# Weight sums spread over the U stage, the first gate pair's front drawn into the last output pair, and a reordered last row in a one-core encoder block

## The chip, the cores and the metric

The kernel runs on one core of one Trainium2 chip. The metric is the device time of one execution in microseconds (us), the median of several executions. TensorE (PE) does the matmuls and transposes, VectorE (DVE) and ScalarE (ACT) the elementwise work, GpSimd (POOL) a few small powers and some table loads, and SyncE (SP) issues nearly all of the 176 MB of DMA.

## The reference, cut to what matters

One layer of an encoder for 512 prompt and 1024 sample rows of width 1024, all in float32:

```python
xn = rmsnorm(h, norm_mix_g)
q, k, v, g_att, u, g_f = split(xn @ w_in)        # six column groups of 512
att = diff_attention(q, k, v, lam, rel_bias)     # 4 heads, softmax(1) - lam * softmax(2)
att = rmsnorm(att, subln_g) * (1 - lambda_init) * silu(g_att)
fno = real(fft2(u per group)) @ w_fourier * silu(g_f)
h = h + concat(att, fno) @ w_out
h = h + sigmoid(rmsnorm(h, ple_norm_g) @ w_ple_gate) * (p @ w_ple_proj)
return rmsnorm(h, final_norm_g)
```

## The kernel before

Every float32 operand of a matmul is split into a high and a low part (`split`, L53: a cast on ACT, a subtraction on DVE), and each product is three matmuls. The 1536 rows are 12 tiles of 128, or three chunks of 512 columns. The Tile framework orders the instructions of each engine from the program's order and its own estimate of times, and gives out the buffers of a tag as they come free, so a load may stand well ahead of its place in the program.

The stages, in order of time:

- V (to about 82 us): the chunks are loaded, and the value columns computed.
- U (82 to 148 us): for each row tile t, 24 matmuls into one of two `acc` banks, an ACT multiply that empties the bank into `u`, and a store. After t = 3, 7, 11 `norm_in_place` (L326) normalizes a chunk (24 DVE and 8 ACT instructions). `combine` (L408) makes sums of weight quarters for a seven-product form of the 2x2 block product: two loads of 512 KB into a tile `wr`, four subtractions into a tile `f`, then for `w_out` (n = 0 to 3) four splits and four stores of `so`, for `w_ple_gate` (n = 4 to 7) two ACT multiplies by the norm's gain and two stores of `sg`. Before, `combine` 0 to 3 follow t = 1, 4, 7, 10.
- The first column blocks of q and k (148 to about 182 us): `columns_on` (L210) is a generator; `run(columns_on, 3)` advances it by one block and chunk, that is 24 matmuls. `blocks` loads the weights of the next block (`load_col`: tags `raw`, `wch`, `wcl`, two buffers each) when it begins a block. `combine` 4 to 7 each follow one of the first four such steps. After six steps the pool `pn` closes, and `pf` takes its memory: `fa` with rows of u, `cs` and `wf` with tables.
- The Fourier stage (to about 290 us), with more columns between its products, then attention (to about 669 us), with columns and the first two output tiles poured between its steps.
- The output projection: tiles 2 to 11 in pairs. `left` (L908) makes the seven left operands of a pair from four blocks `cl`, with temporaries f1, f2 from the tag `tmp` (two buffers, which tiles 0 and 1 use for their split columns `ch`). `project_pair` (L926) does the seven products of 12 matmuls into four banks, adds each to x, and `keep` stores the row and sums its squares, with `acc` banks as ACT's dummy output. At t = 4 the weights `wp` of p and the final gain `gfin` are loaded.
- The gate: `front` (L997) loads a pair of kept rows, normalizes them (`normed`, into a buffer of tag `hn`, which has four; the staging tiles `raw4` of all late weights share the tag), transposes them on PE (L993) and makes the left operands. `front(0)` begins after the last output pair and runs to its end between the loads of the second and third of the seven gate weights. `gate_pair` (L1068) does the products of one pair and the next pair's front; `finish_row` (L1047) ends each row.

In the last row `gfin` is multiplied in ahead of the final scale, in three pieces (L1109, L1116 twice), and the two halves leave through ACT's and SP's queues.

Of the kernel before, what the change touches and what calls it, by code (L numbers as in the profile page):

```python
# [15 lines left out]
D = 1024  # L16
# [16 lines left out]
def block_kernel(ctx, tc, i, yp, ys):  # L33
# [10 lines left out]
    def tr():  # L44
        return psum.tile([P, 512], F32, tag="tr", name="tr", bufs=2)
# [150 lines left out]
    def blocks(*todo):  # L196
# [7 lines left out]
        for n, (b, chunks) in enumerate(todo):  # L204
# [2 lines left out]
            w = nxt  # L207

    ALL = (0, 1, 2)
    columns_on = blocks(("k0 q0", (0, 1)), ("k0 q0", (2,)), ("g0 k1 q1 g1 k2 q2 g2 k3 q3 g3", ALL),  # L210
                        ("f0 f1 f2 f3", (0, 1)))

    def run(gen, n=None):
# [37 lines left out]
    with tc.tile_pool(name="pn", bufs=1, side="right", reuse_waits="tile") as pn:  # L251
# [156 lines left out]
        def combine(n):  # L408
            k, gate = n % 4, n // 4
            src = i["w_ple_gate" if gate else "w_out"][0]  # L410
            both = pn.tile([P, 4, 512], F32, tag="xs" if gate else "wn", name="wr", bufs=4)
            r = [both[:, 0:2], both[:, 2:4]]
            for j in range(2):
                b = 4 * j + k
                nc.sync.dma_start(out=r[j].rearrange("p a b -> p (a b)"), in_=src[b * P:(b + 1) * P, :])
                if gate:
                    nc.scalar.mul(out=r[j], in_=r[j], mul=gcol[:, b:b + 1])
            f = pn.tile([P, 4, 512], F32, tag="wn", name="f", bufs=4)
            t1, t2, t3, t4 = (f[:, z] for z in range(4))
            for out, x0, x1 in ((t1, r[0][:, 1], r[0][:, 0]), (t2, r[1][:, 1], t1),  # L420
                                (t3, r[1][:, 1], r[0][:, 1]), (t4, t2, r[1][:, 0])):
                nc.vector.tensor_tensor(out=out, in0=x0, in1=x1, op=ALU.subtract)
            if gate:
                for z in range(2):
                    nc.sync.dma_start(out=sums_g[z][:, :, k], in_=f[:, 2 * z:2 * z + 2])
            else:
                for m, t in zip(SUMS_R, (t1, t2, t3, t4)):
                    if m in ("t1", "t3"):
                        o2 = pn.tile([P, 4, 512], F32R, tag="wn", name="o", bufs=4)
                    o = o2[:, 0:2] if m in ("t1", "t3") else o2[:, 2:4]  # L430
                    split(o[:, 0], o[:, 1], t)
                    nc.sync.dma_start(out=sums_o[m][:, :, k], in_=o.bitcast(F32))

        wu = load_nat(2048, "xs")
        for t in range(NT):
            c, q = t // 4, (t % 4) * P
            ps = acc()
            for k in range(KB):
                x = [x[c][k // 4][:, k % 4, q:q + P] for x in (xh, xl)]
                mm3(ps, *x, wu[0][k // 4][:, k % 4], wu[1][k // 4][:, k % 4], k == 0, k == KB - 1)  # L440
            s, r = rows_of(t)
            u = px.tile([P, 512], F32, tag="th", name="u", bufs=3)
            nc.scalar.mul(out=u, in_=ps, mul=rs[c][:, t % 4:t % 4 + 1])
            nc.sync.dma_start(out=uu[s][r:r + P, :], in_=u)
            if t % 4 == 3:
                norm_in_place(c, rs[c])
            if t % 3 == 1:
                combine(t // 3)
        for n in range(6):
            run(columns_on, 3)  # L450
            if n < 4:
                combine(4 + n)


    with tc.tile_pool(name="pf", bufs=1, side="right", reuse_waits="tile") as pf:
# [427 lines left out]
    with ExitStack() as pcx:  # L883
# [21 lines left out]
        def add(out, x0, x1, eng=None):  # L905
            (eng or nc.vector).tensor_tensor(out=out, in0=x0, in1=x1, op=ALU.add)

        def left(cl):  # L908
            c11, c12, c21, c22 = cl
            a = {n: halves(n) for n in SUMS}  # L910
            a["11"] = a["11"][0], c11
            f11, f12, f21, f22 = (c.bitcast(F32) for c in cl)
            f1, f2 = tmp(), tmp()
            split(*a["12"], f12)
            split(*a["22"], f22)
            add(f1, f21, f22)
            split(*a["s1"], f1)
            sub(f2, f1, f11)
            split(*a["s2"], f2)
            sub(f2, f12, f2)  # L920
            split(*a["s4"], f2)
            sub(f1, f11, f21)
            split(*a["s3"], f1)
            return a, split_own(*a["11"])

        def project_pair(t, a, x):  # L926
            (xa, xb), L, R = x, slice(0, 512), slice(512, 1024)
            b0, b1, b2, b3 = banks(t)
            product(b0, a["11"], wb["11"], True)
            add(xa[:, L], b0, xa[:, L])  # L930
            product(b2, a["12"], wb["21"], True)
            add(xa[:, L], b2, xa[:, L])
            product(b3, a["22"], wb["t4"], True)
            sub(xb[:, L], xb[:, L], b3)
            product(b1, a["s1"], wb["t1"], True)
            add(xb[:, R], b1, xb[:, R])
            product(b0, a["s2"], wb["t2"], False)
            add(xa[:, R], b0, xa[:, R])
            product(b1, a["s4"], wb["22"], False)
            add(xa[:, R], b1, xa[:, R])  # L940
# [6 lines left out]
        def raw4():  # L947
            return pool.tile([P, D], F32, tag="hn", name="raw", bufs=4)

        a, (hi, lo) = left(pair_cl)  # L950
        with tc.issue_after(hi.ins), tc.issue_after(lo.ins):
            project_end(*later[0])
        for t in range(2, NT, 2):
            if t == 4:
                wp = [[pool.tile([P, D], F32R, tag=f"wp{k}{n}", name=f"wp{k}{n}") for n in "hl"]
                      for k in range(2)]
                gfin = pool.tile([P, D], F32, name="gfin")
                nc.scalar.dma_start(out=gfin, in_=i["final_norm_g"].rearrange(
                    "(a d) -> a d", a=1).broadcast_to([P, D]))
                for k in range(2):  # L960
                    raw = raw4()
                    nc.sync.dma_start(out=raw, in_=i["w_ple_proj"][0][k * P:(k + 1) * P, :])
                    split(*wp[k], raw)
            if t > 2:
                a, _ = left(load_cl(t, True))
            project_pair(t, a, [load_x(t, row(t)), load_x(t + 1, row(t + 1))])

        def rows_in(t):

# [27 lines left out]
        def front(t):  # L997
# [13 lines left out]
            pa = columns(pr, 0)  # L1011
            yield
            gb = normed(t + 1, xb)
            bank = tr if t else acc
            nc.scalar.copy(out=f21, in_=turn(gb, 0, bank()))
            ps = turn(gb, 1, bank())
            split(*a["22"], ps)
            add(f1, f21, ps)
            yield
# [27 lines left out]
        def finish_row(t, u, x, g, ss, n):  # L1047
            x, g, last = x[u], g[u], t + u == NT - 1
            rs = pool.tile([P, 1], F32, tag="rs", name="rs", bufs=2)
            nc.vector.tensor_reduce(out=rs, in_=ss[:, 4 * u:4 * u + n], op=ALU.add, axis=mybir.AxisListType.X)  # L1050
            rpow(rs, rs)
            t += u
            for z in range(2):
                w = slice(512 * z, 512 * z + 512)
                dst = yp[0, t * P:(t + 1) * P, w] if t < 4 else ys[0, (t - 4) * P:(t - 3) * P, w]
                if not last:
                    nc.vector.scalar_tensor_tensor(out=g[:, w], in0=x[:, w], scalar=rs, in1=gfin[:, w],
                                                   op0=ALU.mult, op1=ALU.mult)
                    nc.sync.dma_start(out=dst, in_=g[:, w])
                elif z == 0:  # L1060
                    nc.scalar.mul(out=g[:, w], in_=x[:, w], mul=rs)
                    nc.scalar.dma_start(out=dst, in_=g[:, w])
                else:
                    nc.vector.tensor_scalar(out=g[:, w], in0=x[:, w], scalar1=rs, scalar2=None,
                                            op0=ALU.mult)
                    nc.sync.dma_start(out=dst, in_=g[:, w])

        def gate_pair(t, x, p, g, a):  # L1068
            ahead = front(t + 2) if t + 2 < NT else iter(())
# [151 lines left out]
```

## Time and profile before

| | |
|---|---|
| median of 3 runs | 945.7 us (945.49 to 946.87) |
| the profiled execution: its own time, its span | 947.0 us, 944.9 us |
| PE busy in the span | 903.0 us (96%), 4476 matmuls |
| DVE, ACT, POOL busy | 677.8, 480.3, 93.8 us |
| mean granted PE clock | 0.992 of full speed |
| DMA | 176.14 MB, 186 GB/s over the span |

The span runs from the first to the last instruction; 2.1 us of the profiled execution's own time lie around it. A busy PE is not PE at its peak, since matmuls are pipelined.

### The profile page before, as it was taken

Reading aid. Unit: us, or ns where it says so; the run is one execution under the profiler, and the core shown is the slowest. Engines: PE = TensorE matmul, PEld = TensorE weight load, DVE = VectorE, ACT = ScalarE, POOL = GpSimd, SP = SyncE. Lnnn points to the kernel's source line nnn. Section 1 sums busy time; section 2 is a strip of 40 time slices with the busy share of each in tenths; the row PEclk is TensorE's granted clock in tenths of the full one; section 3 lists DMA queues with packets and bytes.
Section 4 is the critical chain, followed back from the end, with each engine's and each line's share of the span. In section 5 each row is a group of like instructions: output and inputs, shape, how many; then the busy total and the mean of one; then the engine's idle time right before and its main releaser. Section 6 shows DMA issues by size and latency. Waiting matters only on the chain.

```text
span 944.9 us, 13060 instructions
## 1 busy us (share of the span) xinstructions
PE 903.0 (96%) x4476; PEld 741.7 (78%) x4476; DVE 677.8 (72%) x1303; ACT 480.3 (51%) x947; POOL 93.8 (10%) x112
## 2 busy tenths in 40 slices
PE   7999999799999999999999999989999999999995
PEld 6878887578887788888888788778678877888885
DVE  7944888466853698678785986994586778767774
ACT  8833455232333566465564655663434467556552
POOL 0100000200000101101112222431000000000000
PEclk9999999989999999999999999999999999999999
DMA  8459648964536944672659548639985463233301
GB/s 309 148 178 321 237 179 312 347 215 144 157 124 208 243 126 145 159 227 80 186 171 249 171 135 247 214 109 322 346 284 167 156 214 132 101 100 101 101 30 60
DMA packets 125313, 176.14 MB, mean 186 GB/s; under 512 B 9464, under 2 KB 77304, under 8 KB 124224
## 3 DMA queue, kind: packets, MB, share of 16 engines
q1 hardware_dynamic: 123136, 171.25, 56.6%
q0 software_dynamic: 1392, 2.63, 1.1%
q10 hardware_dynamic: 720, 1.44, 0.5%
q8 instruction: 35, 0.57, 0.3%
q14 instruction: 30, 0.25, 0.1%
HBM read 115.48 MB, written 59.80 MB: 186 GB/s over the span
## 4 chain that ended last, share of the span: by engine, by line
PE 75%; DVE 10%; DMA 7%; ACT 3%; issue 2%; POOL 1%; SPq 1%; POOLq 0%; DVEq 0%; ACTq 0%
PE acc L138 22%; PE bank L624 15%; PE sc L760 6%; PE acc L66 5%; PE acc L68 5%; PE acc L67 5%; PE tr L787 3%; PE sc L66 2%; PE sc L67 2%; PE sc L68 2%; DMA raw<-sg 2%; PE tr L66 2%; PE tr L67 2%; DMA raw<-w_in 2%; PE tr L68 2%
## 5 line engine op out<-in xcount | busy, mean ns | idle before, releaser
L138 PE MATMUL acc<-xh,wch 128*128 128x512 f32 x384 | 153.3, 399 | 10.2 <-ACT wch L55 8.9
L138 PE MATMUL acc<-xl,wch 128*128 128x512 f32 x384 | 153.4, 400 | 0.0
L138 PE MATMUL acc<-xh,wcl 128*128 128x512 f32 x384 | 152.7, 398 | 0.0
L766 ACT ACTIVATE pt<-pt,mx 128x1024 f32<-128x1024 f32 (+1 forms) x96 | 96.5, 1007 | 60.5 <-DVE mx L763 58.7
L763 DVE CUSTOM_DVE_ANT_0 pt<-sc,tb 128x1024 f32<-128x1024 f32 (+1 forms) x96 | 97.8, 1040 | 20.0 <-PE sc L760 15.6
L138 PEld LDWEIGHTS acc<-xh,wch 128*128 128x128 f32 x384 | 72.8, 190 | 24.5 <-ACT wch L55 9.3
L138 PEld LDWEIGHTS acc<-xh,wcl 128*128 128x128 f32 x384 | 72.8, 190 | 14.5 <-DVE wcl L59 0.8
L138 PEld LDWEIGHTS acc<-xl,wch 128*128 128x128 f32 x384 | 72.9, 190 | 13.3 <-issue 0.2
L760 PE MATMUL sc<-kk,qq 128*128 128x512 f32 x160 | 65.5, 409 | 1.7 <-DMA qq<-qs_p 1.7
L760 PE MATMUL sc<-kll,qq 128*128 128x512 f32 x160 | 63.8, 399 | 0.0
L55 ACT CAST wth<-tr 128x512 fp32r<-128x512 f32 x80 | 45.5, 582 | 31.4 <-PE tr L787 31.3
L59 DVE TENSOR_TENSOR wtl<-tr,wth 128x512 fp32r<-128x512 f32 x80 | 53.4, 685 | 6.1 <-ACT wth L55 5.8
L782 DVE SCALAR_TENSOR_TENSOR pt<-pt,rc,pt 128x1024 f32<-128x1024 f32 (+1 forms) x48 | 54.4, 1133 | 1.1
L787 PE MATMUL tr<-ident,pt 128*128 128x128 f32 x320 | 48.4, 276 | 6.1 <-DVE g L832 4.1
L808 POOL TENSOR_TENSOR g<-ot,g 128x256 f32<-128x256 f32 x24 | 20.3, 847 | 308.0 <-ACT ot L807 301.6
L66 PE MATMUL acc<-wn,xh 128*128 128x512 f32 x128 | 50.6, 397 | 0.0
L68 PE MATMUL acc<-wn,xl 128*128 128x512 f32 x128 | 50.5, 394 | 0.0
L787 PEld LDWEIGHTS tr<-ident,pt 128*128 128x128 f32 x320 | 36.6, 140 | 17.4 <-DVE g L832 6.4
L67 PE MATMUL acc<-wn,xh 128*128 128x512 f32 x128 | 50.2, 392 | 0.0
L66 PE MATMUL tr<-wth,v 128*128 128x256 f32 x160 | 45.7, 286 | 0.2 <-DVE wtl L59 0.2
L67 PE MATMUL tr<-wtl,v 128*128 128x256 f32 x160 | 45.5, 285 | 0.2 <-DVE wtl L59 0.2
L68 PE MATMUL tr<-wth,v 128*128 128x256 f32 x160 | 45.2, 282 | 0.0
(326 smaller groups left out, 2194.0 us busy)
## 6 DMA issues: line engine op xcount, KB each, us to landing
raw<-w_in SPq DMA_DIRECT2D x29, 512.0 KB, 4.8
sot<-o SPq DMA_DIRECT2D x16, 512.0 KB, 3.6
hs<-x SPq DMA_DIRECT2D x12, 512.0 KB, 4.8
x<-hs SPq DMA_DIRECT2D x12, 512.0 KB, 3.9
xs<-x_cols SPq DMA_DIRECT2D x11, 512.0 KB, 5.9
cl<-cT SPq DMA_DIRECT2D x22, 256.0 KB, 4.1
wr<-w_out SPq DMA_DIRECT2D x8, 512.0 KB, 5.2
wr<-w_ple_gate SPq DMA_DIRECT2D x8, 512.0 KB, 5.0
```

Source lines behind the costliest of these rows:

```text
L55: a = nc.scalar.copy(out=hi, in_=src)
L59: return a, eng.tensor_tensor(out=lo, in0=src, in1=hi.bitcast(F32), op=ALU.subtract)
L66: nc.tensor.matmul(out=out, lhsT=wh, rhs=xh, start=start, stop=False)
L67: nc.tensor.matmul(out=out, lhsT=wh, rhs=xl, start=False, stop=False)
L68: nc.tensor.matmul(out=out, lhsT=wl, rhs=xh, start=False, stop=stop)
L138: nc.tensor.matmul(out=ps, lhsT=a[:, k], rhs=b[c][k // 4][:, k % 4], start=(n == 0), stop=(n == 23))
L624: nc.tensor.matmul(out=out[:, w], lhsT=a[u][:, k], rhs=b[v][:, k, w], start=(start and k == 0 and n == 0), stop=(k == 3 and n == 2), skip_ ...
L760: nc.tensor.matmul(out=pss[c][:, n:n + 512], lhsT=qq[c], rhs=k[c][:, n:n + 512], start=(m == 0), stop=(m == 1))
L763: nc.vector.tensor_tensor_reduce(out=pt[c][:, :T], in0=ps[:, :T], in1=tb[:, off:off + T], scale=-1.0, scalar=3e38, op0=ALU.add, op1=ALU.mi ...
L766: nc.scalar.activation(out=pt[c][:, :T], in_=pt[c][:, :T], func=AF.Exp, scale=-1.0, bias=mx[:, c:c + 1], accum_out=sm[:, c:c + 1])
L782: nc.vector.scalar_tensor_tensor(out=pt[0][:, :T], in0=pt[1][:, :T], scalar=rc[:, 1:2], in1=pt[0][:, :T], op0=ALU.mult, op1=ALU.add)
L787: nc.tensor.transpose(out=ps[:, j * P:(j + 1) * P], in_=pt[0][:, (b + j) * P:(b + j + 1) * P], identity=ident)
```

## The change

The sums are made in the tile that the weights were loaded into, and `f` is gone; the gate's sums leave in four stores of 256 KB instead of two of 512 KB. `combine` 0 to 5 follow t = 1, 3, 5, 7, 9, 11 of the U stage, and 6 and 7 follow the first and fourth column step. The q block is loaded once for all three chunks. The first `left` takes its temporaries from an `hn` buffer. `wp` and `gfin` are loaded at t = 8. `front(0)` runs inside the last output pair (t = 10): its loads ahead of the pair, its row pieces after the third and the sixth kind of product as `project_pair` marks them, its end after the pair; all its transposes use `tr` banks. In the last row the gain is multiplied into the upper half in the final instruction, and into the lower half in one piece after the loop.

```diff
-    columns_on = blocks(("k0 q0", (0, 1)), ("k0 q0", (2,)), ("g0 k1 q1 g1 k2 q2 g2 k3 q3 g3", ALL),
+    columns_on = blocks(("k0", (0, 1)), ("q0", ALL), ("k0", (2,)), ("g0 k1 q1 g1 k2 q2 g2 k3 q3 g3", ALL),
                         ("f0 f1 f2 f3", (0, 1)))
...
         def combine(n):
-            both = pn.tile([P, 4, 512], F32, tag="xs" if gate else "wn", name="wr", bufs=4)
+            both = pn.tile([P, 4, 512], F32, tag="xs" if n > 5 else "wn", name="wr", bufs=4)
...
-            f = pn.tile([P, 4, 512], F32, tag="wn", name="f", bufs=4)
-            t1, t2, t3, t4 = (f[:, z] for z in range(4))
-            for out, x0, x1 in ((t1, r[0][:, 1], r[0][:, 0]), (t2, r[1][:, 1], t1),
-                                (t3, r[1][:, 1], r[0][:, 1]), (t4, t2, r[1][:, 0])):
+            (w11, w12), (w21, w22) = ((x[:, 0], x[:, 1]) for x in r)
+            for out, x0, x1 in ((w11, w12, w11), (w12, w22, w12), (w22, w22, w11), (w21, w22, w21)):
                 nc.vector.tensor_tensor(out=out, in0=x0, in1=x1, op=ALU.subtract)
+            places = {"t1": w11, "t2": w22, "t3": w12, "t4": w21}
             if gate:
-                for z in range(2):
-                    nc.sync.dma_start(out=sums_g[z][:, :, k], in_=f[:, 2 * z:2 * z + 2])
+                for z in range(4):
+                    nc.sync.dma_start(out=sums_g[z // 2][:, z % 2, k], in_=places[SUMS_R[z]])
...
-            if t % 3 == 1:
-                combine(t // 3)
+            if t % 2 == 1:
+                combine(t // 2)
         for n in range(6):
             run(columns_on, 3)
-            if n < 4:
-                combine(4 + n)
+            if n in (0, 3):
+                combine(6 + n // 3)
...
-        def left(cl):
+        def left(cl, first=False):
...
-            f1, f2 = tmp(), tmp()
+            if first:
+                f1, f2 = raw4().rearrange("p (n a b) -> n p a b", n=2, b=P)
+            else:
+                f1, f2 = tmp(), tmp()
...
-        def project_pair(t, a, x):
+        def project_pair(t, a, x, ahead=iter(())):
...
             product(b3, a["22"], wb["t4"], True)
             sub(xb[:, L], xb[:, L], b3)
+            next(ahead, None)
             product(b1, a["s1"], wb["t1"], True)
             add(xb[:, R], b1, xb[:, R])
             product(b0, a["s2"], wb["t2"], False)
             add(xa[:, R], b0, xa[:, R])
+            next(ahead, None)
             product(b1, a["s4"], wb["22"], False)
...
+            return next(ahead, None)
...
-            bank = tr if t else acc
-            nc.scalar.copy(out=f21, in_=turn(gb, 0, bank()))
-            ps = turn(gb, 1, bank())
+            nc.scalar.copy(out=f21, in_=turn(gb, 0, tr()))
+            ps = turn(gb, 1, tr())
...
-                if not last:
+                if not last or z:
                     nc.vector.scalar_tensor_tensor(out=g[:, w], in0=x[:, w], scalar=rs, in1=gfin[:, w],
                                                    op0=ALU.mult, op1=ALU.mult)
                     nc.sync.dma_start(out=dst, in_=g[:, w])
...
-                nc.vector.tensor_tensor(out=xb[:, R], in0=xb[:, R], in1=gfin[:, R], op=ALU.mult)
                 for n in range(2):
...
                     finish_half(1, 0, x, pp, g, ss[:, (4, 6)[n]:(5, 7)[n]], n)
-                    nc.vector.tensor_tensor(out=xb[:, w], in0=xb[:, w], in1=gfin[:, w], op=ALU.mult)
+                nc.vector.tensor_tensor(out=xb[:, L], in0=xb[:, L], in1=gfin[:, L], op=ALU.mult)
...
         for t in range(2, NT, 2):
-            if t == 4:
+            if t == 8:
                 wp = ...
...
-        first = front(0)
-        next(first)
+            x = [load_x(t, row(t)), load_x(t + 1, row(t + 1))]
+            first = front(0) if t == NT - 2 else iter(())
+            next(first, None)
+            nxt = project_pair(t, a, x, first)
         for n, tag in (("11", "x*00"), ("21", "x*10"), ("t4", "t4*"), ("t1", "t1*"), ("t2", "x*01"),
                        ("22", "x*11"), ("t3", "t3*")):
-            if n == "t4":
-                *_, nxt = first
```

## Rows read from the trace of the kernel before

**Rows 1.** Stretches: length, busy PE, PEld, DVE, ACT, POOL (instructions), clock, DMA share, GB/s.

```profile
82.00:148.00 66.00, 66.00 (x295) 54.03 (x294) 49.56 (x82) 26.67 (x45) 0.00 (x0) 1.00 0.67 240
148.00:200.00 52.00, 41.76 (x168) 32.56 (x167) 31.79 (x53) 20.94 (x29) 5.82 (x10) 0.90 0.96 317
```

**Rows 2.** PE's waits: who released it, us in total, times, longest.

```profile
PE acc L138 <- ACT wch L55: 8.9, 1, 8.9
...
PE bank L624 <- DVE x L906: 1.6, 1, 1.6
...
PE acc L138 <- DVE lo L59: 1.3, 1, 1.3
PE bank L624 <- DVE cl L59: 1.3, 1, 1.3
PE bank L624 <- DVE al L59: 0.9, 1, 0.9
```

**Rows 3.** The chain of waits, 160 to 198 us: start, length, what.

```profile
160.10 11.01 PE acc L138 x47
...
174.75 9.80 DMA sg<-f
...
184.99 5.00 DMA raw<-w_in
...
191.12 1.22 PE acc L138 x2
192.37 5.28 PE acc L138 x14
```

**Rows 4.** A stretch of 2 us after PE's longest wait, columns as in rows 1.

```profile
194.00:196.00 2.00, 2.00 (x7) 1.52 (x6) 0.00 (x0) 0.00 (x0) 0.00 (x0) 0.50 0.64 172
```

**Rows 5.** SP's queue in order of time: the load into the second `raw` buffer.

```profile
93.58 0.38 SPq L126 DMA_DIRECT2D raw<-w_in  x1
```

**Rows 6.** DMA issues from 148 to 192 us: count, size, median us to landing.

```profile
sg<-f SPq DMA_DIRECT2D x8, 512.0 KB, 5.4
...
kl_s<-lo SPq DMA_DIRECT2D x2, 256.0 KB, 4.0
...
wf<-w_fourier POOLq DMA_DIRECT2D x1, 256.0 KB, 6.5
```

**Rows 7.** DVE in order of time, around the first output pairs.

```profile
667.92 0.69 DVE L903 TENSOR_TENSOR tmp<-tmp,cl 128x512 f32<-128x512 f32 x1 [4.34 <-PE acc L67]
...
681.29 1.23 DVE L59 TENSOR_TENSOR wp0l<-raw,wp0h 128x1024 fp32r<-128x1024 f32 x1 [2.54 <-ACT wp0h L55]
...
685.53 0.68 DVE L906 TENSOR_TENSOR x<-bank,x 128x512 f32<-128x512 f32 x1
```

**Rows 8.** PE in order of time: its two waits between output and gate.

```profile
772.25 1.27 PE L993 MATMUL acc<-ident,raw 128*128 128x128 f32 x8 [1.71 <-ACT acc L660]
...
795.16 1.09 PE L993 MATMUL tr<-ident,raw 128*128 128x128 f32 x8 [1.44 <-ACT raw L986]
```

**Rows 9.** The chain of waits from 760 us: the first staged sum's load.

```profile
760.02 3.78 DMA raw<-sg
```

**Rows 10.** ACT in order of time: the second row of the first gate pair.

```profile
759.95 1.16 ACT L986 ACTIVATE raw<-x,small 128x1024 f32<-128x1024 f32 x1
```

**Rows 11.** DVE in order of time: the last gate weight's low part.

```profile
796.08 1.23 DVE L59 TENSOR_TENSOR wt3l<-raw,wt3h 128x1024 fp32r<-128x1024 f32 x1 [1.61 <-ACT wt3h L55]
```

**Rows 12.** The end of the span, DVE and ACT in order of time.

```profile
936.82 0.42 ACT L1042 ACTIVATE raw<-raw 128x256 f32<-128x256 f32 x1
937.04 0.68 DVE L1109 TENSOR_TENSOR x<-x,gfin 128x512 f32<-128x512 f32 x1
...
938.31 0.41 DVE L1044 SCALAR_TENSOR_TENSOR x<-raw,x 128x256 f32<-128x256 f32 x1
...
939.30 0.42 DVE L1116 TENSOR_TENSOR x<-x,gfin 128x256 f32<-128x256 f32 x1 [0.57 <-ACT raw L1045]
...
940.70 0.49 DVE L1064 TENSOR_SCALAR raw<-x,rs 128x512 f32<-128x512 f32 x1 [0.72 <-POOL rs L653]
```

More of the change, by code (lines that the diff above doesn't have):

```diff
@@ L417, in combine @@
                     nc.scalar.mul(out=r[j], in_=r[j], mul=gcol[:, b:b + 1])
-            f = pn.tile([P, 4, 512], F32, tag="wn", name="f", bufs=4)
-            t1, t2, t3, t4 = (f[:, z] for z in range(4))
-            for out, x0, x1 in ((t1, r[0][:, 1], r[0][:, 0]), (t2, r[1][:, 1], t1),
-                                (t3, r[1][:, 1], r[0][:, 1]), (t4, t2, r[1][:, 0])):
+            (w11, w12), (w21, w22) = ((x[:, 0], x[:, 1]) for x in r)
+            for out, x0, x1 in ((w11, w12, w11), (w12, w22, w12), (w22, w22, w11), (w21, w22, w21)):
                 nc.vector.tensor_tensor(out=out, in0=x0, in1=x1, op=ALU.subtract)
+            places = {"t1": w11, "t2": w22, "t3": w12, "t4": w21}
             if gate:
-                for z in range(2):
-                    nc.sync.dma_start(out=sums_g[z][:, :, k], in_=f[:, 2 * z:2 * z + 2])
+                for z in range(4):
+                    nc.sync.dma_start(out=sums_g[z // 2][:, z % 2, k], in_=places[SUMS_R[z]])
             else:
-                for m, t in zip(SUMS_R, (t1, t2, t3, t4)):
+                for m, t in places.items():
                     if m in ("t1", "t3"):
@@ L906, in add, with raw4 @@
             (eng or nc.vector).tensor_tensor(out=out, in0=x0, in1=x1, op=ALU.add)
-        def left(cl):
+        def raw4():
+            return pool.tile([P, D], F32, tag="hn", name="raw", bufs=4)
+        def left(cl, first=False):
             c11, c12, c21, c22 = cl
@@ L945, in project_pair @@
                 keep(t + u, x[u])
[L947 to L953, printed above, removed]
-            if t == 4:
[L955 to L966, printed above, removed]
+            return next(ahead, None)
         def rows_in(t):
@@ L1059, in finish_row @@
                     nc.sync.dma_start(out=dst, in_=g[:, w])
-                elif z == 0:
+                else:
                     nc.scalar.mul(out=g[:, w], in_=x[:, w], mul=rs)
                     nc.scalar.dma_start(out=dst, in_=g[:, w])
[L1063 to L1066, printed above, removed]
         def gate_pair(t, x, p, g, a):
@@ L1115, in gate_pair @@
                     finish_half(1, 0, x, pp, g, ss[:, (4, 6)[n]:(5, 7)[n]], n)
-                    nc.vector.tensor_tensor(out=xb[:, w], in0=xb[:, w], in1=gfin[:, w], op=ALU.mult)
+                nc.vector.tensor_tensor(out=xb[:, L], in0=xb[:, L], in1=gfin[:, L], op=ALU.mult)
             finish_row(t, 1, x, g, ss, 3 if last else 2)
             return next(ahead, None)
-        first = front(0)
-        next(first)
+        a, (hi, lo) = left(pair_cl, True)
+        with tc.issue_after(hi.ins), tc.issue_after(lo.ins):
+            project_end(*later[0])
+        for t in range(2, NT, 2):
+            if t == 8:
+                wp = [[pool.tile([P, D], F32R, tag=f"wp{k}{n}", name=f"wp{k}{n}") for n in "hl"]
+                      for k in range(2)]
+                gfin = pool.tile([P, D], F32, name="gfin")
+                nc.scalar.dma_start(out=gfin, in_=i["final_norm_g"].rearrange(
+                    "(a d) -> a d", a=1).broadcast_to([P, D]))
+                for k in range(2):
+                    raw = raw4()
+                    nc.sync.dma_start(out=raw, in_=i["w_ple_proj"][0][k * P:(k + 1) * P, :])
+                    split(*wp[k], raw)
+            if t > 2:
+                a, _ = left(load_cl(t, True))
+            x = [load_x(t, row(t)), load_x(t + 1, row(t + 1))]
+            first = front(0) if t == NT - 2 else iter(())
+            next(first, None)
+            nxt = project_pair(t, a, x, first)
         for n, tag in (("11", "x*00"), ("21", "x*10"), ("t4", "t4*"), ("t1", "t1*"), ("t2", "x*01"),
                        ("22", "x*11"), ("t3", "t3*")):
-            if n == "t4":
-                *_, nxt = first
             w = wblock(n, tag)
```

## The prediction

> **What bounds the kernel now.** I read the page first: PE is busy for 903.0 of 944.9 us, so a change that leaves PE's work as it is can win only from the 41.9 us in which PE stands, and from PE's slow stretches. Then I asked for the busy time by stretches: in the U stage PE is busy all the time, with DVE idle for 16.4 of 66 us and the DMA engines used for two thirds; in the next 52 us, with DMA at 0.96, PE stands for 10.2 us and its clock falls [rows 1]. PE's waits name the places: one of 8.9 us for a weight's cast, then small ones for DVE in the first output pairs [rows 2], and two at the seam between output and gate [rows 8]. Last I followed the chain of waits through the long one: a store of sums takes 9.80 us to land, the load of a weight (g's first block) is issued only at 184.99, behind other stores in SP's queue, lands after 5.00, is cast, and PE starts at 191.12 [rows 3]. The reader is to see that the columns up to there are not late: PE's last matmul of the q block ended 8.9 us before, at 182.2.
>
> **The long wait.** After it PE runs at a granted clock of 0.50, its lower level of 1.2 GHz [rows 4]; ahead of the wait it was at full clock. 48 matmuls at full clock took 11.01 us, 0.229 each; the 16 after the wait run from 191.12 to 197.65, 6.53 where 3.67 would do [rows 3]. So this place costs 8.9 + 2.9 = 11.8 us. Both halves of the edit take it away. With q loaded once, the order of loads is k0, q0, k0, g0, and g0 is the fourth; before it was the fifth. The fourth load of before was issued at 93.58, some 90 us ahead of its use, because its `raw` buffer was free [rows 5]; g0 takes that place, out of SP's crowd. Its split needs q0's `wch`, free after the fifth column step, one step (24 x 0.229 = 5.5 us) ahead of g0's first matmul. The load after it, k1, waits for the second k0's split and is needed only three chunks (16.5 us) after g0's start. I take the whole 11.8; if another block's weight were as late, nothing would be won.
>
> **The spread sums.** No addition is saved: 4 subtractions per `combine` before and after. Two gate sums (4 DMA loads of 512 KB, 2 MB of stores, 4 ACT multiplies, 8 subtractions) go from the crowded stretch to the U stage, with q's second load gone altogether. 8 subtractions at 0.68 [rows 7] are 5.4 us in 16.4 idle ones, and ACT is busy for 26.7 of 66 [rows 1]: hidden, cost 0. What stands behind a late ACT multiply is the emptying of `acc`; with two banks of 5.5 us each PE loses only what goes beyond some 4.8 us. The 1.3 us that PE waits for k0's low part [rows 2] stay: it stands in DVE's queue behind the third chunk's norm, in both kernels. Bounds: it could go (+1.3), or `combine` 5, now ahead of it in the program, could put four subtractions before it (4 x 0.68 = -2.7).
>
> The gate's sums leave in 16 stores of 256 KB and no longer in 8 of 512 KB. In the crowded stretch 512 KB took 5.4 us to land and 256 KB 4.0 [rows 6]; nothing PE needs at once stands behind them, so I take 0. Against the split speaks a rule of the Trainium skill (DMA: Bandwidth & Descriptors, Anatomy of one DMA): a transfer costs about 2.0 us fixed plus its bytes at 436 GB/s, fitted on the GpSimd path. By it the 8 extra stores would be an estimated 16 us of DMA time if they stood in a row; the trace's ratio of 4.0 to 5.4 leans the same way, and it goes into the first rival below.
>
> **The first left operands.** f1 and f2 in `tmp` wait for tile 1's split columns: at 667.92 DVE had stood for 4.34 us on PE with the rest of `left` behind it, and PE then waits 0.9 and 1.3 for parts that come out of that queue [rows 2, 7]. An `hn` buffer lies on memory that attention gave up earlier. DVE gets 4 us more for these pieces: +2.1, lower bound 0.
>
> **p's weights.** The next wait, 1.6 us [rows 2], is for an addition at 685.53; DVE had stood 2.54 us for `wp`'s cast at 681.29, and the pair's additions queued behind it [rows 7]. With `wp` at t = 8, its loads may go behind those of the second pair (+1.6), or the framework may issue them early all the same. Then the addition comes when it came, and PE, 2.1 earlier, waits that much longer: -2.1. I take +0.5, nearer the upper end, since a later place lowers its priority.
>
> **The front in the last pair.** PE's 16 transposes move, they don't go. What goes is PE's wait of 1.71 at 772.25: the second eight used `acc` banks that `keep`'s squares held [rows 8]; now they use `tr` banks inside the pair. Their data are there: the second row was normalized at 759.95 [rows 10], and its place, one product ahead of the pair's end, is 772.25 - 1.71 - 1.03 (eight transposes) - 12 x 0.229 = 766.8. The x rows were loaded early before, too. ACT's and DVE's pieces go into a pair where both have some idle time. The other wait, 1.44 at 795.16, belongs to the chain of gate weights: the next pair's norm waits for an `hn` buffer, which the last weight's staging holds [rows 8, 11]. I leave it: +1.7; with it +3.1. The lower bound is the second rival.
>
> **The last row.** Ahead of the second quarter's addition at 938.31, the multiply at 937.04 (0.68) and a quarter's (0.41) go; but that quarter's tanh ends at 936.82 + 0.42 = 937.24, and one short step stands between it and the addition, so about 0.7 of the 1.0 is won. After the square a multiply of 512 columns (0.68) takes the place of one of 256 (0.42): 0.26 back. The final instruction on DVE grows from 0.49 to about 0.68, beside ACT's half, which is no shorter [rows 7, 12]. +0.4; bounds 0.2 and 1.0 (the multiply behind the sum of squares).
>
> **Sum.** 11.8 + 2.1 + 0.5 + 1.7 + 0.4 = 16.5 us. The profiled execution's span goes from 944.9 to 928.4, its own time from 947.0 to 930.5; its own time is 1.3 above the median of 945.7, so the median goes to **929.2**. Attention between has other small waits of PE, which I leave as they are.
>
> **Rivals.** *First, tables behind the sums.* `pf` takes `pn`'s memory, so `fa`, `cs` and `wf` now wait for `combine` 6's and 7's stores out of the `xs` tiles themselves. PE wants the tables 11.8 us earlier, at 197.65 - 11.8 = 185.9 [rows 3]. If `combine` 7 is made only after its place in the program (q0's second chunk, about 171), its stores leave at about 177; landing as slowly as 9.8 and the table's load at 6.5 [rows 3, 6] make 193.3: 7.4 us of waiting. Against it: a 256 KB store took 4.0 in the crowd [rows 6], and of its 16.5 MB (317 GB/s for 52 us [rows 1]) 4.5 are gone. Time: 929.2 + 7.4 = 936.6. The fixed cost per transfer that the Trainium skill states (DMA: Bandwidth & Descriptors, Anatomy of one DMA) would feed this case.
>
> *Second, the staging ring turns against the change.* The four `hn` buffers hold both rows of the front until the gate pair ends; the weights have the other two. Before, the first four staged weights lay in the ring long before the rows. If the ring now serves in program order, the rows come first, and no gate weight is loaded until the second row's norm. Ten staged tiles took from 760.02 to 797.31 through two buffers, 3.73 each [rows 9, 11]; fourteen take 52.2. From 760 that ends at 812.2, 14.9 later than before: 929.2 + 1.7 + 14.9 = 945.8, no change. Every us by which the row comes after 760 makes it slower; at its place in the program, 766.8, the time is 952.6. From 760 on it decides. Against it: loads took free buffers far ahead of their place before [rows 5].
>
> *Third, the gate weights keep their time.* They are ready at 797.31 as before, and PE, ahead by 2.1 + 0.5 + 1.7, stands for them: 929.2 + 4.3 = 933.5. For it: they were nearly late before [rows 8, 11]; against it, their chain starts when the last output pair frees its weights, so it moves along with PE but for the 1.7.
>
> *Fourth, the change doesn't do what it says*: the crowd only moves, and another weight or a chunk's norm holds PE for as long: 929.2 + 11.8 = 941.0.
>
> **How the numbers follow.** Forecast 0.64; first rival 0.12; second 0.06 (half unchanged, half slower); third 0.12; fourth 0.06. All upper ends together give 945.7 - (11.8 + 1.3 + 2.1 + 1.6 + 3.1 + 1.0) = 924.8. The forecast alone lies within 925 to 932; with the first and third rivals 924.5 to 937.5, which leaves out under 2 in 10. About 0.2% (1.9 us) is what a measurement can tell from no change. Faster 0.93, within it 0.03, slower 0.04 (the second rival's late case, with a little for waits unseen).
>
> **What would show it.** The long wait gone from PE's list, no half clock near 190 us, g0's load issued near 94 us, and `combine` 4 and 5 on DVE before 148. The waits of 0.9 and 1.3 at the first pair gone, the first subtraction into f2 some 4 us before PE ends tile 1; no DVE wait for `wp`'s cast ahead of the second pair. One seam wait fewer, transposes among the last pair's products. Wrong would be: PE waiting on `sc` for a table near 186 us, the first w_ple_gate staging loads after 755 us, or a new wait in the U stage for ACT's emptying.

## The result, and the profile after

The changed kernel takes **953.2 us** (median of 6 runs, 951.79 to 956.83) against 946.86 of the kernel before on the same chip (6 runs, 945.49 to 948.41): a ratio of 1.0069, with an interval of 1.0051 to 1.0088. It is slower by 0.7%, where 929.2 was forecast. The profiled execution took 951.79, its span 949.9, 5.0 more than before; the medians lie 6.3 apart.

PE's waits in two stretches of the changed kernel, from 60 to 300 us and from 650 to 830 (releaser, us in total, times, longest), answer to [rows 2, 8]:

```profile
PE acc L138 <- DVE lo L59: 4.0, 1, 4.0
PE tr L517 <- DVE fyl L59: 2.6, 1, 2.6
...
PE bank L624 <- ACT wt4h L55: 2.0, 1, 2.0
PE bank L624 <- DVE wt2l L59: 1.5, 2, 0.8
PE bank L624 <- DVE al L59: 1.4, 1, 1.4
PE bank L624 <- ACT wt3h L55: 1.1, 1, 1.1
PE bank L624 <- DVE cl L59: 1.1, 1, 1.1
...
PE bank L624 <- DVE wt4l L59: 0.8, 1, 0.8
PE bank L624 <- DVE wt1l L59: 0.8, 1, 0.8
PE bank L624 <- DVE wt3l L59: 0.8, 1, 0.8
PE bank L624 <- DVE w22l L1142: 0.6, 2, 0.3
PE bank L624 <- ACT w22h L1141: 0.5, 1, 0.5
```

The long wait for `wch` is gone. In its place stand 4.0 for k0's low part (`lo`: PE waits for the bank that DVE reads for it) and 2.6 for `fyl`, the low part of what the Fourier stage makes first from `fa`. Both seam waits are gone, and the eight rows of waits for gate weights (w22, wt1 to wt4) are new, 8.1 us together. They lie in the first gate pair. This is SP's queue in the changed kernel, the staging loads of p's and the gate's weights:

```profile
672.71 1.06 SPq L1114 DMA_DIRECT2D raw<-w_ple_proj  x1
...
752.00 0.94 SPq L1135 DMA_DIRECT2D raw<-w_ple_gate  x2
...
771.51 0.32 SPq L1135 DMA_DIRECT2D raw<-sg  x1
```

This is the first gate load of before:

```profile
683.28 0.42 SPq L1136 DMA_DIRECT2D raw<-w_ple_gate  x1
```

Before, four gate loads went out between 683.28 and 699.30, and the first load after them was that of a sum, at 760.02 [rows 9]. Now the first gate load leaves at 752.00, after the first row's norm, although none of the four buffers held anything from 688.7 on, when the cast of p's second weight ended (687.49 + 1.22 on DVE). The chain of waits then runs from load to cast to low part to the next load, as [rows 9, 11] show it for the last weight alone:

```profile
771.51 4.50 DMA raw<-sg
...
776.03 1.05 ACT wt4h L55
...
777.11 1.24 DVE wt4l L59
...
778.36 3.15 DMA raw<-sg
...
794.93 3.58 DMA raw<-sg
...
798.53 1.05 ACT wt3h L55
...
799.61 1.24 DVE wt3l L59
...
800.89 1.45 PE bank L624 x5
```

Each next load waits until the low part before it is made (778.35) and its buffer is free (778.36). The last low part, at 796.08 in [rows 11], comes at 803.05:

```profile
803.05 1.23 DVE L59 TENSOR_TENSOR wt3l<-raw,wt3h 128x1024 fp32r<-128x1024 f32 x1 [0.89 <-ACT wt3h L55]
```

The same stretches as in [rows 1], then two slow ones, after the two new waits (columns as there):

```profile
82.00:148.00 66.00, 66.00 (x296) 54.30 (x295) 52.89 (x85) 28.87 (x47) 0.00 (x0) 1.00 0.75 269
148.00:200.00 52.00, 45.41 (x189) 36.70 (x188) 32.90 (x61) 19.72 (x29) 5.80 (x10) 0.93 0.90 284
160.00:164.00 4.00, 2.96 (x7) 2.41 (x8) 4.00 (x8) 2.59 (x4) 0.00 (x0) 0.58 0.96 330
196.00:198.00 2.00, 2.00 (x8) 1.71 (x8) 0.82 (x2) 0.58 (x1) 0.00 (x0) 0.50 0.89 269
```

DVE works more in U and DMA is a little less full behind it, as forecast; but PE gains 3.65 us of work in the 52. Its clock no longer falls near 191, but it falls twice: near 161, behind the 4.0, and near 195, behind the 2.6. By the granted clock (0.58 from 160 to 164, 0.70 from 194 to 196, 0.50 from 196 to 198) the two stretches cost an estimated 4 x 0.42 + 2 x 0.30 + 2 x 0.50 = 3.3 us, no less than the 2.9 that the prediction counts behind the long wait.

Where the 5.0 came from, by marks that both kernels pass on PE (after minus before): first column matmul (147.66 to 145.93) -1.7; from there to the first scores, "stretch A", 151.7 to 147.3, -4.5; on to the last output pair's first product +1.6; from there to the end of the second gate pair, "stretch B", 77.5 to 87.0, **+9.5**; the rest +0.1. Most of the first gain is no part of the change: PE is 1.0 ahead already in the V stage (30.86 against 31.84 at its first product into `acc`). In stretch A, PE's waits give 4.7: 8.9, 1.3 and 1.7 before (the last for a load of q, ahead of the first scores), 4.0, 2.6 and 0.6 now. The stretch from the first scores to the last output pair took 449.7 to 454.3 in the fourteen profiles of this document, so that the 1.6 says nothing. In stretch B the last output pair became shorter, 21.15 where it was 23.24, and the first gate pair went from 28.41 to 39.19. Profiles of one code differ too: stretch A was 147.3 to 150.0 in four profiles with the changed kernel's early code.

### The profile page after: what moved, and what is told of

Read it like the earlier page. It is cut to its first block, busy times and chain, and to the rows that moved or that the text cites. A ratio compares the mean times of both kernels' runs of the same rounds, so it can differ in the third digit from the quotient of the medians.

```text
span 949.9 us, 13050 instructions
## 1 busy us (share of the span) xinstructions
PE 907.0 (95%) x4476; PEld 743.1 (78%) x4476; DVE 677.3 (71%) x1300; ACT 479.9 (51%) x946; POOL 94.7 (10%) x112
## 4 chain that ended last, share of the span: by engine, by line
PE 77%; DVE 8%; DMA 8%; ACT 3%; issue 2%; SPq 1%; POOL 1%; POOLq 0%; DVEq 0%; ACTq 0%
PE acc L138 22%; PE bank L624 15%; PE sc L760 6%; PE acc L66 5%; PE acc L67 5%; PE acc L68 5%; PE tr L787 3%; PE sc L66 2%; PE sc L67 2%; PE sc L68 2%; PE tr L66 2%; PE tr L67 2%; PE tr L68 2%; DMA raw<-sg 2%; PE tr L509 1%
## 5 line engine op out<-in xcount | busy, mean ns | idle before, releaser
L55 ACT CAST wth<-tr 128x512 fp32r<-128x512 f32 x80 | 45.5, 582 | 31.6 <-PE tr L787 31.5
L66 PE MATMUL tr<-wth,v 128*128 128x256 f32 x160 | 45.7, 285 | 0.2 <-DVE wtl L59 0.2
L59 DVE TENSOR_TENSOR wcl<-raw,wch 128x1024 fp32r<-128x1024 f32 x21 | 26.5, 1262 | 27.2 <-ACT wch L55 23.5
```

The costliest lines, as they stand in the source:

```text
L55: a = nc.scalar.copy(out=hi, in_=src)
L59: return a, eng.tensor_tensor(out=lo, in0=src, in1=hi.bitcast(F32), op=ALU.subtract)
L66: nc.tensor.matmul(out=out, lhsT=wh, rhs=xh, start=start, stop=False)
```

## The experiments

All times beside a run are compared with the kernel before on the same chip, as a ratio with its interval. "A" and "B" are the two stretches just named, from the profile.

| run | median us | ratio | A | B |
|---|---|---|---|---|
| before, after (profiles above) | 946.9, 953.2 | 1.0069 | 151.7, 147.3 | 77.5, 87.0 |
| front_back | 946.5 | 0.998 (0.995 to 1.001) | 148.7 | 77.1 |
| weights_first | 944.9 | 0.996 (0.993 to 0.998) | 150.0 | 76.8 |
| two_rings | 948.1 | 1.000 (0.997 to 1.002) | 149.1 | 81.2 |
| front_only | 958.2 | 1.009 (1.006 to 1.013) | 150.6 | 89.4 |
| cols_only | 943.7 | 0.994 (0.992 to 0.997) | 146.6 | 78.0 |
| sums_only | 948.2 | 1.001 (0.998 to 1.003) | 151.4 | 77.3 |
| all_sums_in_u | 947.1 | 1.000 (0.998 to 1.002) | 151.9 | 76.2 |
| five_later | 941.4 | 0.991 (0.989 to 0.994) | 146.7 | 77.0 |
| old_left | 939.9 | 0.992 (0.990 to 0.993) | 144.7 | 76.8 |
| cols_staged | 943.3 | 0.995 (0.993 to 0.998) | 145.4 | 79.1 |
| cols_staged_fa | 942.3 | 0.995 (0.993 to 0.997) | 146.6 | 79.8 |
| **fa_early** | **935.9** | **0.989 (0.988 to 0.991)** | 139.5 | 76.9 |

### The ring: four runs on stretch B

**front_back**: the changed kernel with the front at its old place.

```diff
-            nc.scalar.copy(out=f21, in_=turn(gb, 0, tr()))
-            ps = turn(gb, 1, tr())
+            bank = tr if t else acc
+            nc.scalar.copy(out=f21, in_=turn(gb, 0, bank()))
+            ps = turn(gb, 1, bank())
...
-            first = front(0) if t == NT - 2 else iter(())
-            next(first, None)
-            nxt = project_pair(t, a, x, first)
+            project_pair(t, a, x)
+        first = front(0)
+        next(first)
...
+            if n == "t4":
+                *_, nxt = first
```

> The changed kernel with the first gate pair's front put back at the seam (begun after the last output pair, ended between the second and third gate weight, acc banks for the second row); all other parts of the change stay. Theory: in the changed kernel the staging ring is served in program order, so the rows of the front stand ahead of the gate weights, whose loads start at 752 instead of 683, and gate pair 0 loses 11.6 us to that. Then here the loads start near 680 again, the waits of about 8 us in gate pair 0 go, and the time is that of before less the 4.6 us by which the changed kernel's PE was ahead in the output pairs: about 942. Rival (the loss comes from the rest of the change, from moved sums or p's weights or DMA traffic): the time stays near 953.

**weights_first**: the front stays in the last pair, behind the first two gate weights (`gate_raw` loads a staged half, `gate_split` casts it; the loop behind the pair keeps the other five).

```diff
+        def staged_front():
+            raws = [(n, k, gate_raw(n, k)) for n in ("11", "21") for k in (0, 2)]
+            rest = front(0)
+            next(rest)
+            yield
+            new = {n: wblock(n, tag) for n, tag in (("11", "x*00"), ("21", "x*10"))}
+            for n, k, raw in raws:
+                gate_split(n, k, new[n], raw)
+            yield from rest
...
-            first = front(0) if t == NT - 2 else iter(())
+            first = staged_front() if t == NT - 2 else iter(())
...
```

> The changed kernel with the front still inside the last output pair, but the four staged halves of the first two gate weights loaded ahead of the front's rows and cast inside the pair, after its third product and ahead of the first row's norm. Theory (order in the ring): the loads go out before 700, only ten staged tiles are left for two buffers, and the time is 942 less the seam's wait of 1.7, about 940 to 942. Rival (a front inside the last pair costs ACT and DVE time there, whatever the ring does): the pair gets longer by the casts, 4.6 us of ACT, and the time is 945 or more.

**two_rings**: rows and staging in rings of their own.

```diff
-            hn = raw4()
+            hn = pool.tile([P, D], F32, tag="hr" if t % 4 < 2 else "hn", name="hn", bufs=2)
...
-            return pool.tile([P, D], F32, tag="hn", name="raw", bufs=4)
+            return pool.tile([P, D], F32, tag="hn", name="raw", bufs=2)
```

> The changed kernel with the hn ring cut in two of two buffers each: the rows of pairs 0, 4 and 8 have one ring, the staged weights and the rows of pairs 2, 6 and 10 the other. Memory and the places in the program stay. Theory (order): the rows no longer stand ahead of the weights, the first two staged halves are loaded long before 752, and the waits of gate pair 0 go nearly all: 940 to 944. Rival (number of buffers: fourteen tiles through two buffers is too slow wherever they start, 52 us): gate pair 0 keeps half of its 8 us of waits or more, 948 to 953.

**front_only**: the kernel before with the four edits of the front alone (`project_pair`'s `ahead`, `tr` banks, the call inside t = 10, no call at the seam).

> The kernel before with only the first gate pair's front moved into the last output pair. Theory (order in the ring): slower by what gate pair 0 lost in the changed kernel, 11.6, less the seam's 1.7 to 3: 946.9 + 9 = about 956. Rival (the front is harmless by itself, and the loss needs the sums in 256 KB stores or p's weights at t = 8): 944 to 947.

The gate's first loads in SP's queue, in front_back:

```profile
684.04 0.94 SPq L1138 DMA_DIRECT2D raw<-w_ple_gate  x2
...
759.06 8.19 SPq L1138 DMA_DIRECT2D raw<-sg  x4
```

in weights_first:

```profile
683.01 0.94 SPq L1110 DMA_DIRECT2D raw<-w_ple_gate  x2
```

in two_rings:

```profile
687.36 0.38 SPq L1135 DMA_DIRECT2D raw<-w_ple_gate  x1
693.57 0.37 SPq L1135 DMA_DIRECT2D raw<-w_ple_gate  x1
755.49 0.38 SPq L1135 DMA_DIRECT2D raw<-w_ple_gate  x1
```

and in front_only, with the waits of PE that follow:

```profile
755.38 0.94 SPq L1137 DMA_DIRECT2D raw<-w_ple_gate  x2
```

```profile
PE bank L624 <- ACT wt4h L55: 2.5, 1, 2.5
PE bank L624 <- DVE wt2l L59: 1.5, 2, 0.8
```

Order in the ring decides. Wherever the front's rows ask for `hn` buffers ahead of the gate weights, the first gate load leaves after 750; where the weights ask first, at 683, with the front in the same place. In two_rings the rows still stand ahead of the weights in the program, with SP's loads for them (751.17, 756.42), so it was the shared ring that held the weights, and not SP's queue. The sentence ahead of the prediction, that a tag's buffers are given out as they come free, is thus true only in the order in which the program asks for them. front_only has the whole loss by itself: B is 89.4, 11.9 longer than before, and the waits are those of the changed kernel. two_rings tells order from number: with two buffers for staging, the first two loads leave at 687 and B falls from 87.0 to 81.2. So 5.8 of the 9.5 us go with the order alone. The other 3.7, beside before, stay where only two of the four early loads have a buffer (the third leaves at 755.49); that the number of buffers is their cause is argued from this, since no run changes the number alone.

The times lie 3 to 5 us above what I expected of front_back and weights_first, in part because the early stage gave less in their profiles (A 148.7 and 150.0), and two_rings fell between its two theories, as the 5.8 and 3.7 say.

The seam's own gain is small: weights_first has B at 76.8, only 0.3 under front_back and 0.7 under before. Its time, 944.9, lies at the edge of its rival's 945, but the pair did not get longer by the casts, as that rival had it: the last output pair takes 21.15, as in the changed kernel, 2.1 less than before. The two gate pairs behind it take 28.88 and 27.91, where they took 28.41 and 27.06, 1.3 more. Its waits in the first gate pair (wt3l 0.8, w22h 0.6, wt3h 0.2) are what the prediction's third rival said: the weights keep their time.

### The early stage: sums, columns and fa

**cols_only** is before with the new `columns_on` line; **sums_only** is before with the new `combine` and its new places.

> The kernel before with the q block loaded once for all three chunks, and nothing else. In the changed kernel g's first weight was loaded at 92.05 and the long wait of 8.9 was gone, but PE reached the Fourier products only 5.1 us earlier, since fyl came late (the load of fa from uu_p took 9.22). Theory one (the order of loads took the long wait away, the crowd of sums then holds fa): g's first load near 93, no long wait at 182, but the four sums still leave between 160 and 190, so fa is issued near 190 or later and PE waits for fyl or for the tables up to about 200: gain 0 to 4 us, Fourier products from 220 to 224. Rival (the order of loads is the whole gain): no wait at fyl, Fourier products near 213, time 935 to 937.

> The kernel before with the sums made in place and spread over the U stage, the q block still loaded twice. Theory one: g's first load is the fifth and waits for a raw buffer until the cast near 171 to 175, with less in SP's queue ahead of it, so PE's long wait shrinks from 8.9 to between 0 and 4; the wait for k0's low part grows from 1.3 to 4.0 as in the changed kernel, because the sums of combine 5 stand in DVE's queue; gain in all 1 to 5 us. Rival (spread sums are free, the prediction's view): the wait for k0's low part stays at 1.3 and the gain is 9 us less what is left of the long wait.

PE's waits from 60 to 300 us, in cols_only and then in sums_only:

```profile
PE tr L517 <- ACT fyh L55: 3.9, 1, 3.9
PE acc L138 <- DVE lo L59: 2.0, 2, 1.3
```

```profile
PE tr L517 <- ACT fyh L55: 4.1, 1, 4.1
PE acc L138 <- DVE lo L59: 4.0, 1, 4.0
```

Either half alone takes the 8.9 away: no `wch` stands in either list. Both meet 4 us for `fyh` instead. The columns gain 5.1 in A, a little over the 0 to 4 expected; the sums gain nothing that can be measured (1.001), since they add 2.7 at k0's low part, and PE's waits at `fyh` and `fyl` are 4.8 us there. The rival of each is refuted: the columns aren't worth 10, and the sums aren't free.

**five_later** and **all_sums_in_u** move the sums, both on weights_first. In five_later, `combine` 5 also takes its `wr` from `xs`:

```diff
-            if t % 2 == 1:
+            if t % 2 == 1 and t < 11:
                 combine(t // 2)
...
-            if n in (0, 3):
-                combine(6 + n // 3)
+            if n in (0, 2, 3):
+                combine(5 + (0, 2, 3).index(n))
```

and, with `AT = (0, 1, 3, 4, 5, 7, 8, 9)`, no `combine` behind U and every `wr` in `wn`:

```diff
-            if t % 2 == 1:
-                combine(t // 2)
+            if t in AT:
+                combine(AT.index(t))
```

> The version with the weights staged first, with combine 5 after the first column step (ahead of 6, which now follows the third, and 7 after the fourth) and no longer after the last row tile. Theory: the four subtractions of combine 5 no longer stand ahead of k0's low part, and PE's wait there falls from 4.0 to about 1.3 to 2; the stores leave later, so fyl's wait grows by 1 to 3 and takes the gain back: 943 to 946. Rival (the wait for k0's low part is the norm's own and not the sums'): it stays near 4.

> The version with the weights staged first, and all eight sums made inside the U stage (after row tiles 0, 1, 3, 4, 5, 7, 8, 9), none behind the third norm. Theory (the 4.0 us for k0's low part and the 3 us for fyl come from sums that stand behind U): the first goes back to 1.3, fa is issued a few us earlier and lands in less than 6, the wait for fyl goes; time 938 to 940. Rival (DVE has no room in U): PE waits in the U stage for banks of acc, the columns start 2 to 5 us later, and nothing or less than nothing is won: 944 or more.

In five_later the wait for k0's low part is 1.4 and that for `fyh` 3.9; the time, 941.4, is better than expected. all_sums_in_u takes 947.1, the rival's time. One wait has swallowed the rest, with DVE's queue behind it:

```profile
PE acc L138 <- DVE lo L59: 12.0, 1, 12.0
```

```profile
151.77 0.69 DVE L421 TENSOR_TENSOR wr<-wr 128x512 f32<-128x512 f32 x1 [2.23 <-ACT wr L417]
...
169.29 0.69 DVE L59 TENSOR_TENSOR lo<-acc,hi 128x512 fp32r<-128x512 f32 x1
```

Three of the subtractions stand for their ACT multiply (2.23, 1.79 and 1.12), with the third norm and `lo` queued behind them. PE didn't wait inside U, as the rival had it, but right behind it. `fyl`'s wait did go.

**fa_early** is five_later with the first block of u's rows loaded into a `th` buffer; **cols_staged** is before with the columns and `staged_front` alone, and **cols_staged_fa** that with the early load.

```diff
+        fa0 = px.tile([P, 4, P], F32, tag="th", name="fa0", bufs=3)
+        nc.sync.dma_start(out=fa0, in_=uu["p"].rearrange("(j p) c -> p j c", p=P)[:, :, 0:P])
         for n in range(6):
             run(columns_on, 3)
...
+            if (s, g) == ("p", 0):
+                a = fa0
+            else:
+                a = pf.tile([P, KB, P], F32, tag="fa", name="fa", bufs=2)
```

> The version with combine 5 after the first column step, and the first block of u's rows for the Fourier stage (fa of group 0) loaded into a th buffer of the column pool right after the U stage, so that it waits neither for pn's memory nor behind the stores of the column steps. Theory (PE's 3 to 4 us at fyl or fyh come from this one load, 8.5 to 10.8 us to land): the wait goes or falls under 1, PE keeps its clock there, and the Fourier products come 4 to 5 us earlier: 941.4 - 4 = 936 to 938. Rival (the tables or the second load are as late): PE waits for the next of them nearly as long, 940 to 942.

> The kernel before with two things only: the q block loaded once, and the first gate pair's front in the last output pair with the first two gate weights staged ahead of its rows. Theory (the gains are these two, and add): 943.7 of the columns alone less 1.8 to 3 at the seam, 941 to 942. Rival (the seam is lost again in gate pair 0, whose weights keep their time): 943.5 or more.

> The version with the q block loaded once and the gate weights staged first, with the sums as in the kernel before, and fa of group 0 loaded early as well. Theory: PE waits next for the tables of the Fourier stage, which were wanted at 195 in the version with the columns alone, or for wf, so 1 to 3 us are won and not 4: 938 to 941. Rival (fa was the only late one): as much won as in the version with spread sums, 937 to 938.

The chain of waits in the changed kernel shows what that load waits for:

```profile
177.49 0.58 SPq L425
...
178.11 2.98 DMA sg<-wr
181.09 0.68 DVE lo L155
...
182.98 0.53 SPq L462
...
183.56 9.22 DMA fa<-uu_p
...
194.50 0.88 PE tr L517 x4
```

A sum's store lands, DVE makes a low part of q, SP issues the stores of q that are queued ahead, then `fa`, which takes 9.22. Whether `fa` waited longer for its memory or for the queue can't be told from this; the next run takes both away. In fa_early the load is issued, in SP's queue, at

```profile
147.87 0.63 SPq L450 DMA_DIRECT2D fa<-uu_p  x1
```

and the wait is gone: 1.5 for `lo`, 0.4 at a later product and 0.2 for q are all that PE waits up to the first scores. A falls by 7.2 against five_later, more than the wait's 3.9. The clock gives an estimated 2.3 (12 us at 0.81 from 196 to 208 in five_later, 1.00 from 148 to 220 here), the load of q ahead of the first scores 1.1 (1.3 to 0.2). But these are the slowest execution of five_later and the fastest of fa_early: by the medians the load is worth 5.5, and beside old_left (below), which has five_later's early code, 4.0. 935.9 beats both kernels, by 1.1% the one before. With the old sums the same load gives 942.3, more than the 938 to 941 expected, and PE waits 3.4 for `cwl`, which is made from the tables `cs` and `wf`: there the tables are as late as `fa`. cols_staged came out at 943.3, just under its rival's 943.5: the seam isn't won (B 79.1). In both runs the first gate pair is longer than in old_left, 31.5 and 31.9 where that takes 28.9: in cols_staged the clock fell (last section), in cols_staged_fa it stayed at 1.00 and PE waited 3.6 us, 3.0 of them for gate weights. Why these two are longer stays open.

### The first left operands and p's weights

**old_left** is five_later with both edits undone.

```diff
-        a, (hi, lo) = left(pair_cl, True)
+        a, (hi, lo) = left(pair_cl)
...
-            if t == 8:
+            if t == 4:
                 wp = ...
```

> The version with combine 5 after the first column step, with the first left operands' temporaries back in tmp and p's weights back at t = 4. Theory (DVE's queue is held by the norm's product that waits for PE, ahead of all of left's work, so the buffers gain nothing, and p's weights gain nothing either): the same time within 1 us, and the first pair's waits 0.8 and 1.2 against 1.4 and 1.1. Rival (the prediction's): slower by 2 to 3 us.

The time is no different (0.992 beside 0.991), though the two ratios together are known only to some 2.6 us, which is what the two edits were to bring. PE's waits of 0.9 (al) and 1.2 (cl) beside 1.4 and 1.1 of the changed kernel say it more clearly: the two edits gain nothing. DVE in the changed kernel shows why (answers to [rows 7]):

```profile
663.09 0.48 DVE L832 SCALAR_TENSOR_TENSOR g<-tr,gs,g 128x256 f32<-128x256 f32 x1 [4.86 <-PE tr L830]
663.49 0.68 DVE L906 TENSOR_TENSOR raw<-c 128x512 f32<-128x512 f32 x1
```

The buffer is free, but the last attention norm stands ahead in DVE's queue and waits 4.86 for PE; the first sum comes right behind it.

## Why the prediction was wrong

**The step that failed** is "The front in the last pair", with the chance given to the second rival: it was put at +1.7, and stretch B, where it lies, lost 9.5 (11.9 in front_only). The rival described what happened: rows first, fourteen staged tiles through two buffers. It put their stretch at 52.2 us; measured, from 752.00 to 803.05 + 1.23, it is 52.3. It had +0.1 to +6.9 beside the 945.7 of before, and +6.3 came. One thing differs: the first two loads left after the first row's norm (752.00), and not after the second's. The argument against it was a load that "took free buffers far ahead of [its] place" [rows 5]. That was true and said nothing: that load was the next in its ring. [Rows 9, 10] fitted both readings, for the four early gate loads stand ahead of the rows in program order too. I gave 0.06 to the side that the program's order spoke for. The near match of the total is partly chance: the rival built on 16.5 - 1.7 = 14.8 us of other gains that mostly didn't come, and its loss was larger than the 9.5 measured.

It is not the only step that failed. front_back has all of the change but the front, for which the sum had 14.8; it won 1.0 (0.998, an interval that holds 1). In the two profiles 21.5 us lie between the forecast and the result: 11.2 at the seam (1.7 + 9.5), 7.3 up to the first scores (11.8 - 4.5), 4.2 from there to the last output pair (2.1 + 0.5, and 1.6 that lie within the spread of profiles), 0.5 behind it, less the 1.7 ahead of the first columns that no term has.

**The long wait**, 11.8: mechanism right, size wrong. g's first weight was loaded at 92.05, as forecast, and the wait and its slow stretch at 191 went. What came to stand next was the first rival's place, at a smaller price: not the tables but `fa`, and 2.6 to 4 us instead of 7.4. The 2.9 for the slow clock came back too, behind the two new waits (an estimated 3.3). Stretch A gained 4.5 in the changed kernel's profile; cols_only alone gains 5.1. I had weighed a forecast and a rival as alternatives where the one leads into the other.

**The spread sums**, 0: the lower bound was the value. On DVE two of `combine` 5's subtractions and the norm's last two splits now stand ahead of k0's low part: 4.0 against 1.3, that is -2.7, and a slow stretch after it (0.58 from 160 to 164). The bound had four subtractions there, so that it came out to the tenth is partly luck. The halved stores cost nothing visible: twelve of 256 KB took a median of 3.4 from 148 to 192, beside 4.0 in [rows 6], and the stretch's DMA share fell from 0.96 to 0.90. By the fixed cost per transfer in the Trainium skill (DMA: Bandwidth & Descriptors, Anatomy of one DMA) a larger cost was to be feared; no run here halves the stores alone.

**The first left operands**, +2.1, and **p's weights**, +0.5: the wait behind DVE's 4.34 was put down to the buffer, but was that of the queue; 0. p's loads went out early in spite of their place (672.71), and the time from the first output pair's first product to the last pair's is 82.7, before 82.0. old_left bears out both.

**The last row**, +0.4: its terms cancel. From PE's last matmul to the sum of squares it takes 4.0 instead of 4.3, the final instruction 0.75 instead of 0.49, and the tail from PE's last matmul to the end is 9.7 against 9.5 before. These lines answer to [rows 12]:

```profile
943.62 0.69 DVE L1098 TENSOR_TENSOR x<-x,gfin 128x512 f32<-128x512 f32 x1 [0.57 <-ACT raw L1032]
944.23 0.15 DVE L1037 TENSOR_REDUCE rs<-ss 128x1 f32<-128x3 f32 x1
...
945.28 0.75 DVE L1044 SCALAR_TENSOR_TENSOR raw<-x,rs,gfin 128x512 f32<-128x512 f32 x1 [0.72 <-POOL rs L653]
```

**Left open**: why PE's clock fell in cols_staged and not in old_left (below), why the first gate pair is longer in cols_staged_fa, and whether the 3.7 that two_rings leaves are the number of buffers.

## What to carry to other kernels

Where tiles share a ring of buffers in this framework, whoever asks first in the program is served first, and those behind stay unloaded even while buffers stand free: before a consumer is moved ahead, list the ring's requests in their new order, and move the loads with it. When a long wait goes, the gain ends at the next late arrival: look for what PE needs next and when that lands, and count only up to there. An early buffer gains nothing while another instruction that waits stands ahead in the same engine's queue.

## What the hardware showed that was not expected

PE's clock can fall or hold after nearly equal pauses. In cols_staged PE waited 0.96 and 0.76 us between 784 and 788 and then ran at its lower level of 1.2 GHz; in old_left it waited 0.68 and 0.76 at the same place, and the granted clock stayed at 1.00 over the whole pair. It stayed there too in five_later, after 0.88 and 0.76 between 790 and 793, and in fa_early, after 0.73 and then 1.22 between 778 and 784. These two stretches are from cols_staged:

```profile
786.00:788.00 2.00, 1.24 (x5) 0.89 (x5) 1.97 (x3) 1.19 (x2) 0.00 (x0) 0.94 0.23 92
788.00:790.00 2.00, 2.00 (x8) 1.61 (x8) 1.13 (x2) 1.07 (x2) 0.00 (x0) 0.50 0.00 0
```

So the price of a pause is not proportional to it: all of PE's waits in this pair are 2.2 us in cols_staged and 1.7 in old_left, but the pair took 31.5 against 28.9. Of the 2.6 between them, 0.5 are waits and an estimated 1.7 the clock (0.94, 0.50 and then 0.71 in three stretches of 2 us).
